# Another order for the half-size products of neighbouring units, and their follow-up work queued some products later

## The chip, the cores and the metric

The kernel is one program on one core of one Trainium2 chip. The metric is the device time of one execution in microseconds, from three runs; the profile is of one further execution. The engines are TensorE (PE in the profile, with its weight loads as PEld), VectorE (DVE), ScalarE (ACT), GpSimd (POOL) and SyncE (SP), which here issues all DMAs. Each engine takes its instructions in the order in which they stand.

## What is computed

One layer of an encoder block on 1024 tokens of width 2048, all in float32:

```python
h = rmsnorm(x, norm_w)
proj = einsum('bsd,de->bse', h, w_in)                # 2048 -> 5632
q_a, k_a, v_a, g_a, q_r, k_r, v_r, g_r = split(proj)
attn = windowed_attention(q_a, k_a, v_a, sink, rel_bias)   # 16 heads, +-128 tokens
attn = rmsnorm(attn, attn_out_norm_w) * silu(g_a)
ret = bidirectional_retention(rotary(q_r), rotary(k_r) * 64 ** -0.5, v_r, decays)  # 8 heads
ret = head_groupnorm(ret, ret_gn_w) * silu(g_r)
x = x + einsum('bse,ed->bsd', concat(attn, ret), w_out)    # 2048 -> 2048
out = rmsnorm(x, final_norm_w)
```

## The kernel before

**Two-part operands.** Every large matmul is done in three: each operand is split into a high part (`wh`, a cast by ACT) and the rest (`wl`, a subtraction, by POOL for the input weights and by DVE for the output weights), and high x high, high x low and low x high are added up in PSUM.

**Stages.** The work of PE stands in this order: six plain units (keys, values and queries of attention, list `STD`), 16 units with the half-size products (list `FAST`: per retention head pair `qk` and `vr`, four gates `ga` of attention, four gates `gr` of retention), done twice, and the output projection in eight column blocks. A unit is 256 output columns for all 1024 tokens. `q` counts the units of the second stage from 0 to 31: for `q` under `NF` = 16 the first half of the 2048 inputs, with the four results (tiles `e`, tags `e11` to `e22`) stored to `yd` in DRAM; from 16 on the second half, with the stored result loaded again as the start (`partial`).

**The half-size products.** A unit's 512 x 1024 half problem is done by seven products of half size (`p` = 0 to 6) instead of eight. Each is 12 matmuls (`multiply`): four rows of `hT`, which hold sums of the input made earlier (`combine`) and read back (`c_load`, `c_split`), times a weight block of 512 x 128. The blocks are the four raw ones (`raws`, loaded by `raw_load`) and their sums (`prep_sums`, on POOL in the first half and on DVE in the second); `prep` splits them. Products 0, 2, 4 and 5 accumulate in one PSUM bank (a, `psMa`), which is read after each; product 1 has bank b, and 3 and 6 have bank c (both `psMb`). `collect` reads a bank into a result tile `e`, by ACT or, in the second half, by an addition on DVE. `slots` lists the products of neighbouring units in turn:

```python
for qq, p in ((q, 0), (q - 1, 4), (q, 1), (q - 1, 6), (q, 2), (q - 1, 5), (q, 3)):
```

In the loop over `slots`, `prep` and `prep_sums` run two and three products ahead, then come `multiply`, `collect` and what is in the list `later`. A bank cannot take the next product before its reader is done.

**Follow-up work.** When a result is complete, `deliver` treats it by kind: a gate gets its SiLU on ACT, a `qk` block is rotated (a shuffle and two multiplications, on DVE and POOL, and an addition, functions `rope` and `add`), a `vr` block is transposed by PE (`to_tokens`). All are stored to DRAM (`gd`, `rqk`, `vrd`). The last two wait in `later` for one product.

**Other work in between.** Behind each three matmuls of the main work (and three of the plain and output units) `point()` counts on and takes steps of other work, at a pace in points: from `jobs` one step of attention or retention, from `aux` steps of smaller work, and it issues stores that are due. Attention (`attn_job`, four groups of four heads) starts in the last plain unit. Retention (`ret_job`, four head pairs) starts in unit `q` = 18; its steps contain the state scans (`kv`: many short DVE additions on `ST`) and the group norm (`o_mm`, `o_fin`). With it starts the premix (`premix`), which multiplies attention's rows by their norm and gate. In the last unit `mixed_load` and `mixed_row` begin to fill `hT` with the rows of the output projection.

Of the kernel before, what the change touches and what calls it, by code (L numbers as in the profile page):

```python
# [36 lines left out]
def hybrid_block(ctx: ExitStack, tc: tile.TileContext, a: dict, out: bass.AP):  # L37
# [93 lines left out]
    def w_low():  # L131
        return wp.tile([128, 512], F32R, tag="wl", name=nm("wl"), bufs=4)
# [66 lines left out]
    def w_load(i):  # L199
        if i < n_w[0] and i not in wraw and i not in wsp:  # L200
            r = et_(("e11", "e21")[i % 2] if i < W_STD else ("e11", "e22", "e21", "e12")[i % 4])
            SP.dma_start(r, w_src(i))
            wraw[i] = r
# [29 lines left out]
    pt, due, pace, adue, apace = [0], [0], [2.9], [0], [2.0]  # L233
# [260 lines left out]
    def attn_job(g):  # L494
# [47 lines left out]
        for t in range(32 + 8):  # L542
            if t < 32:
                b, c = divmod(t, 2)
                pr, n = divmod(b, 8)
                head = 4 * g + 2 * pr + c
                m0, m1 = max(n - 1, 0), min(n + 2, 8)
                W, k0 = 128 * (m1 - m0), 128 * (m0 - n + 1)
                q = qj[b // 2][:, c, 128 * (n % 2) : 128 * (n % 2) + 128]
                p = pS()  # L550
                T.matmul(p[:, :W], q, kh[:, 128 * m0 : 128 * m1], start=True, stop=False)
                T.matmul(p[:, :W], q, kl[:, 128 * m0 : 128 * m1], start=False, stop=True)  # L552
                if c == 0:
                    st[b] = tuple(small(2, w, 4) for w in ("nmx", "sums"))
                nmx, sums = st[b]

                x = att.tile([128, 388], F32, tag="P", name=nm("P"), bufs=5)
                V.tensor_copy(x[:, W : W + 1], nsink[:, head : head + 1])
                P[t] = x
                V.tensor_tensor_reduce(  # L560
                    x[:, :W], p[:, :W], bias[2 * pr + c][:, k0 : k0 + W], -1.0, nsink[:, head : head + 1],
                    ALU.add, ALU.min, nmx[:, c : c + 1],
                )
                A.activation(  # L564
                    x[:, : W + 1], x[:, : W + 1], AF.Exp, bias=nmx[:, c : c + 1], scale=-1.0, accum_out=sums[:, c : c + 1]
                )
                if c == 0 and b:
                    normalise(b - 1)
                if t in (4, 16):
                    load_bias(2 if t == 4 else 3)  # L570
                if t % 4 == 0 and t + 4 < 32:
                    q_load(t // 4 + 1)
            if t == 32:
                normalise(15)
            if t >= 6 and t % 2 == 0 and (t - 6) // 2 < 16:
# [9 lines left out]
                u = out_of(att, [128, 2, 128], F32, "u", 3)  # L585
# [3 lines left out]
            if t >= 4 and t - 4 < 32:  # L589
# [15 lines left out]
                tt(V, lo[:, :nk, c, :], p3, hi[:, :nk, c, :].bitcast(F32), ALU.subtract)  # L605
            yield

    def attn_sum(g):

        for kk in (2 * g, 2 * g + 1):  # L610
            for hf in range(2):
# [4 lines left out]
                yield  # L616
                yield
# [30 lines left out]
    def ret_job(p):  # L648
# [74 lines left out]
        def q_dec(ah):  # L723
            x = r4("qs")
            src = rq[64 * ah : 64 * ah + 64, :].rearrange("p (c i) -> p c i", c=8)
            for d in range(2):
                tt(G if d else V, x[64 * d : 64 * d + 64, :].rearrange("p (c i) -> p c i", c=8), src,
                   qd[64 * ah : 64 * ah + 64, d : d + 1, :].to_broadcast([64, 8, 128]), ALU.mult)
            QS[ah] = x

        def o_mm(ah, h, part):
# [3 lines left out]
            for c in (0, 1) if part == 0 else (2, 3):  # L735
                n = 4 * h + c
                T.matmul(o[:, 128 * c : 128 * c + 128], SD[ah, h][:, c, :], vsl(n, ah),
                         start=(c == 0), stop=False, skip_group_check=True)
                T.matmul(o[:, 128 * c : 128 * c + 128], QS[ah][:, 128 * n : 128 * n + 128],
                         ST[ah][:, 128 * n : 128 * n + 128], start=False, stop=True, skip_group_check=True)  # L740
# [15 lines left out]
        def o_fin(ah, h):  # L756
# [4 lines left out]
            stt(V, t, mv2[:, :, 0], -1.0, y, ALU.mult, ALU.mult)  # L761
            for c in range(4):
# [14 lines left out]
        for todo in (  # L777
            ((k_tr, 0), (q_dec, 0)),
# [9 lines left out]
            ((s_t, 1, 0),),  # L788
            ((o_fin, 0, 0), (o_mm, 0, 1, 0)),
            ((o_mm, 0, 1, 1),),  # L790
            ((o_tr, 0, 0), (kv, 1, 0), (q_dec, 1)),
            ((kv, 1, 1),),
            ((o_fin, 0, 1),),
            ((s_t, 1, 1),),
            ((o_tr, 0, 1),),
            ((o_mm, 1, 0, 0),),
            ((o_mm, 1, 0, 1),),
            ((o_mm, 1, 1, 0),),
            ((o_fin, 1, 0), (o_mm, 1, 1, 1)),
            (),  # L800
            ((o_tr, 1, 0), (o_fin, 1, 1)),
# [15 lines left out]
    def premix(kk):  # L817

        for hf in range(2):
# [4 lines left out]
            SP.dma_start(n, rbd[:, sl])  # L824
            yield
            yield
            tt(G, g, g, n, ALU.mult)
            yield
            yield
            stt(V, r, r, ew[:, kk : kk + 1], g, ALU.mult, ALU.mult)  # L830
            store(md[128 * kk : 128 * kk + 128, sl], r, r, (lambda: done.add(("pre", kk))) if hf else None)

    def mixed_load(kk, hf):
# [6 lines left out]
        mixing.append((kk, hf, r, g))  # L840

    def mixed_row():
        kk, hf, r, g = mixing.popleft()
        if g is not None:
            stt(V, r, r, ew[:, kk : kk + 1], g, ALU.mult, ALU.mult)
        row = 16 * hf + kk
        if row >= 28:
            omix[row] = (rt(F32R), rt(F32R))
        split(orow(row, 0), orow(row, 1), r)
# [32 lines left out]
    def c_split(r):  # L882
        split(hT[:, r, 0:512], hT[:, r, 512:1024], held(staged.pop(r), NT2))
# [37 lines left out]

    for u, (kind, i) in enumerate(STD):
        if u == 2:
            drain(aux, "rows")
        banks = [pS(), pS(), pT(), pO()] if u in (2, 4) else pM()
        st = []
        last_u = u == NS - 1
        for pos in range(NK):
# [21 lines left out]
            if last_u and pos >= 2:  # L950
                for r in range(2 * pos - 6, 2 * pos - 4):
                    if r >= 0:
                        c_split(r)
                for r in range(2 * pos - 4, 2 * pos - 2):
                    c_load(0, r)
            wh, wl = wsp[wi]
            first, last = pos == 0, pos == NK - 1
            for b in range(4):
                p = banks[b]
# [28 lines left out]

    raws, sums, ready_w, banks, outs = {}, {}, {}, {}, {}

    def raw_load(q, names):
        if q < 2 * NF:
            for x in names:
                raws[q, x] = rt(F32)
                SP.dma_start(raws[q, x], a["w_fast"][q, x])


    loads = {}
    for q in range(2 * NF):
        loads[q, 2], loads[q, 4] = [(q + 1, (0, 1))], [(q + 1, (2, 3))]  # L1000


    def prep_sums(q, p):
        eng = V if q >= NF else G
        if p == 2:
            s1, s2 = rt(F32), rt(F32)
            sums[q] = (s1, s2)
            tt(eng, s1, raws[q, 2], raws[q, 3], ALU.add)
            tt(eng, s2, s1, raws[q, 0], ALU.subtract)
        elif p == 4:  # L1010
            w2 = raws[q, 2]
            tt(eng, w2, raws[q, 0], w2, ALU.subtract)

    def prep(q, p):
        src = {0: raws[q, 0], 1: raws[q, 1], 4: raws.get((q, 2)), 5: raws.get((q, 3))}.get(p)
        if src is None:
            src = sums[q][0 if p == 3 else 1]
        hi, lo = wpair(q)
        split(hi, lo, src, G)
        ready_w[q, p] = (hi, lo)  # L1020
        if p == 2:

            tt(V if q >= NF else G, src, raws[q, 1], src, ALU.subtract)
        for at, names in loads.get((q, p), ()):
            raw_load(at, names)

    def multiply(q, p):
        if p in (0, 1, 3):
            banks[q, "abc"[(0, 1, 3).index(p)]] = psum("Ma" if p == 0 else "Mb", 2)
        bank = banks[q, {0: "a", 2: "a", 4: "a", 5: "a", 1: "b", 3: "c", 6: "c"}[p]]  # L1030
        wh, wl = ready_w.pop((q, p))
        for j in range(4):
            ws = slice(128 * j, 128 * j + 128)
            hh, hl = hT[:, 4 * p + j, 0:512], hT[:, 4 * p + j, 512:1024]
            T.matmul(bank, wh[:, ws], hh, start=(j == 0 and p in (0, 1, 3)), stop=False, skip_group_check=True)  # L1035
            T.matmul(bank, wh[:, ws], hl, start=False, stop=False, skip_group_check=True)  # L1036
            T.matmul(bank, wl[:, ws], hh, start=False, stop=(j == 3), skip_group_check=True)  # L1037
            point()

    later = deque()  # L1040

    def partial(q, b):

        if (q, b) not in outs:
            outs[q, b] = et_(("e11", "e12", "e21", "e22")[b])
            if q >= NF:
# [402 lines left out]
```

## Time and profile before

| | us |
|---|---|
| median of 3 runs | 1596.42 |
| lowest, highest | 1590.24, 1601.55 |
| the profiled execution | 1595.88 |
| its span in the profile | 1594.1 |
| mean granted PE clock | 0.975 |

The page of the profile gives the span, each engine's busy time and its share of it, the waits (who stood idle, and whose work ended the wait), and groups of instructions by line, engine, operation and tiles. The numbers behind names are left out there, so `psMb` is each tile of that tag. Most operations are recorded in small helpers (`tt` is L153, `stt` L156, the cast in `split` L159), so it is the tiles' names that tell them apart. L1035 to L1037 are the three matmuls of `multiply`, L1126 the transposes of `to_tokens`.

### The profile page before, as it was taken

The page shows a single profiled execution, that of the slowest core. Times are in us where ns is not written, and L with a number is a line of the kernel's source. Part 1 is how long each engine was busy: PE and PEld are TensorE (multiplying, and loading weights), DVE is VectorE, ACT ScalarE, POOL GpSimd, SP SyncE. Part 2 cuts the span into 40 slices and gives each one's busy share as a digit, 9 for nine tenths or more (in the row PEclk, how much of TensorE's full clock was granted, in tenths as well). Part 3 has the DMA queues.
Part 4 walks back from the last instruction along what each step waited for, and adds up shares of the span by engine and source line. Part 5 has one row for each costly group of instructions (what it writes and reads, how often), then busy time and mean ns, then how long its engine had stood idle before and what let it go on. Part 6 is the DMA issues. An engine that isn't in the chain of part 4 may idle for free. (4 is left out here: it accounts for less than half of the span.)

```text
span 1594.1 us, 21805 instructions
## 1 busy us (share of the span) xinstructions
PE 1484.5 (93%) x7250; PEld 1237.2 (78%) x7250; DVE 923.5 (58%) x1880; ACT 668.1 (42%) x1417; POOL 591.0 (37%) x457
## 2 busy tenths in 40 slices
PE   8999998999999999998888698879998999999997
PEld 6998877887888888887777577657777787887886
DVE  6655446854564664577747856867667444364323
ACT  5311136764675675774332232222353343333210
POOL 3232221446556556445645545554442000113000
PEclk9999999999999999999999899989999999999999
DMA  8888668775455556357774675675464565566413
GB/s 302 300 268 296 243 187 276 244 235 161 139 160 154 159 162 189 115 160 247 242 232 142 201 242 175 219 252 163 155 230 150 173 224 185 159 206 199 135 35 106
DMA packets 195405, 311.73 MB, mean 196 GB/s; under 512 B 29355, under 2 KB 67243, under 8 KB 194652
## 3 DMA queue, kind: packets, MB, share of 16 engines
q1 hardware_dynamic: 195292, 310.33, 60.0%
q8 instruction: 57, 0.93, 0.3%
q14 instruction: 56, 0.46, 0.1%
HBM read 216.38 MB, written 93.88 MB: 195 GB/s over the span
## 5 line engine op out<-in xcount | busy, mean ns | idle before, releaser
L153 POOL TENSOR_TENSOR wl<-r,wh 128x512 fp32r<-128x512 f32 x224 | 298.7, 1337 | 318.9 <-ACT wh L159 308.3
L159 ACT CAST wh<-r 128x512 fp32r<-128x512 f32 x224 | 138.3, 619 | 194.4 <-PE psMa L1036 82.7
L1035 PE MATMUL psMa<-hT,wh 128*128 128x512 f32 x512 | 213.1, 416 | 5.8 <-DVE e L153 4.0
L1037 PE MATMUL psMa<-hT,wl 128*128 128x512 f32 x512 | 201.7, 394 | 2.3 <-POOL wl L153 2.3
L1035 PE MATMUL psMb<-hT,wh 128*128 128x512 f32 x384 | 166.0, 432 | 38.8 <-DVE e L153 38.7
L1036 PE MATMUL psMa<-hT,wh 128*128 128x512 f32 x512 | 201.0, 393 | 0.0
L159 ACT CAST wh<-e 128x512 fp32r<-128x512 f32 x160 | 97.9, 618 | 216.7 <-PE psMb L1254 78.7
L153 DVE TENSOR_TENSOR wl<-e,wh 128x512 fp32r<-128x512 f32 x112 | 84.6, 761 | 132.4 <-ACT wh L159 127.9
L1036 PE MATMUL psMb<-hT,wh 128*128 128x512 f32 x384 | 157.6, 410 | 0.0
L1037 PE MATMUL psMb<-hT,wl 128*128 128x512 f32 x384 | 157.2, 409 | 0.0
L153 POOL TENSOR_TENSOR wl<-e,wh 128x512 fp32r<-128x512 f32 x48 | 71.9, 1501 | 203.8 <-ACT wh L159 203.8
L1035 PEld LDWEIGHTS psMb<-hT,wh 128*128 128x128 f32 x384 | 77.4, 202 | 56.0 <-issue 32.2
L1035 PEld LDWEIGHTS psMa<-hT,wh 128*128 128x128 f32 x512 | 96.9, 189 | 24.6 <-issue 3.4
L1037 PEld LDWEIGHTS psMa<-hT,wl 128*128 128x128 f32 x512 | 96.7, 189 | 24.4 <-POOL wl L153 2.7
L560 DVE CUSTOM_DVE_ANT_0 P<-psST,bias,nsink 128x384 f32<-128x384 f32 (+1 forms) x128 | 74.1, 580 | 62.7 <-PE psST L552 62.4
L1036 PEld LDWEIGHTS psMa<-hT,wh 128*128 128x128 f32 x512 | 97.3, 190 | 16.0
L153 DVE TENSOR_TENSOR PTl<-psST,PTh 128x384 fp32r<-128x384 f32 (+1 forms) x128 | 66.7, 521 | 45.5 <-ACT PTh L604 42.4
L153 POOL TENSOR_TENSOR r<-r,r 128x512 f32<-128x512 f32 x64 | 85.0, 1329 | 20.8 <-DMA yd<-e 6.7
L159 ACT CAST hT<-t 128x512 fp32r<-128x512 f32 x100 | 60.6, 620 | 72.0 <-DMA t<-in_w_out 25.5
L1037 PEld LDWEIGHTS psMb<-hT,wl 128*128 128x128 f32 x384 | 76.8, 200 | 17.7
L564 ACT ACTIVATE P<-P,nmx 128x385 f32<-128x385 f32 (+1 forms) x128 | 76.1, 594 | 30.5 <-DVE nmx L560 28.9
L153 DVE TENSOR_TENSOR e<-psMb,e 128x512 f32<-128x512 f32 x96 | 65.6, 686 | 38.9 <-PE psMb L1037 32.4
(335 smaller groups left out, 3530.3 us busy)
## 6 DMA issues: line engine op xcount, KB each, us to landing
r<-in_w_fast SPq DMA_DIRECT2D x128, 256.0 KB, 2.8
e<-in_w_out SPq DMA_DIRECT2D x112, 256.0 KB, 2.9
yd<-e SPq DMA_DIRECT2D x64, 256.0 KB, 2.9
e<-yd SPq DMA_DIRECT2D x64, 256.0 KB, 3.5
t<-in_xT SPq DMA_DIRECT2D x31, 512.0 KB, 6.1
t<-cd SPq DMA_DIRECT2D x56, 256.0 KB, 4.3
e<-in_w_in SPq DMA_DIRECT2D x48, 256.0 KB, 4.7
md<-t SPq DMA_DIRECT2D x48, 256.0 KB, 2.8
```

The source lines that it names most:

```text
L153: eng.tensor_tensor(o, x, y, op)
L159: A.copy(o_hi, x)
L560: V.tensor_tensor_reduce(x[:, :W], p[:, :W], bias[2 * pr + c][:, k0 : k0 + W], -1.0, nsink[:, head : head + 1], ALU.add, ALU.min, nmx[:, c ...
L564: A.activation(x[:, : W + 1], x[:, : W + 1], AF.Exp, bias=nmx[:, c : c + 1], scale=-1.0, accum_out=sums[:, c : c + 1])
L1035: T.matmul(bank, wh[:, ws], hh, start=(j == 0 and p in (0, 1, 3)), stop=False, skip_group_check=True)
L1036: T.matmul(bank, wh[:, ws], hl, start=False, stop=False, skip_group_check=True)
L1037: T.matmul(bank, wl[:, ws], hh, start=False, stop=(j == 3), skip_group_check=True)
```

## The change

The order of products within `slots` changes, with the order of `FAST`. Each bank is now read right behind its product (c after 3, where it had been read together with a after 4). `prep` and what is queued run in the middle of a product (`between`), and a queue with due slots (`lag`, `run_later`) replaces `later`. Weight sums are formed in place in three parts, at products 0, 6 and 4, with raw loads one by one. The premix moves to POOL; the rows of the output projection are gated by POOL and scaled by ACT's cast. An attention step begins with its last parts, a retention step is cut finer, and the paces become 2.7 (attention) and 2.75 with 2.3 for small work (retention). Some tiles have another number of buffers.

```diff
-FAST = []
-for _p in range(4):
-    FAST += [("qk", _p), ("vr", _p)]
-    FAST += [("ga", 2 * _p), ("ga", 2 * _p + 1)] if _p < 2 else []
-FAST += [("gr", _p) for _p in range(4)]
+FAST = [("ga", 0), ("qk", 0), ("vr", 0), ("qk", 1), ("vr", 1), ("ga", 1), ("qk", 2), ("vr", 2)]
+FAST += [("qk", 3), ("vr", 3), ("ga", 2), ("ga", 3)] + [("gr", _p) for _p in range(4)]
...
-        return out_of(com, [128, 512], F32, tag, 2 if tag == "e12" else 1)
+        return out_of(com, [128, 512], F32, tag, 2 if tag in ("e11", "e12") else 1)
...
-        return wp.tile([128, 512], dt, tag="r", name=nm("r"), bufs=8)
+        return wp.tile([128, 512], dt, tag="r", name=nm("r"), bufs=9)
...
-        return wp.tile([128, 512], F32R, tag="wl", name=nm("wl"), bufs=4)
+        return wp.tile([128, 512], F32R, tag="wl", name=nm("wl"), bufs=3)
...
-    pt, due, pace, adue, apace = [0], [0], [2.9], [0], [2.0]
+    pt, due, pace, adue, apace = [0], [0], [2.7], [0], [2.0]
...
             tt(G, g, g, n, ALU.mult)
-            yield
-            yield
-            stt(V, r, r, ew[:, kk : kk + 1], g, ALU.mult, ALU.mult)
+            tt(G, r, r, g, ALU.mult)
+            yield
...
+        if part == 0:
+            sums[q] = rt(F32)
+            tt(eng, raws[q, 0], raws[q, 0], raws[q, 2], ALU.subtract)
+            tt(eng, sums[q], raws[q, 3], raws[q, 0], ALU.subtract)
+        elif part == 1:
+            tt(eng, raws[q, 2], raws[q, 2], raws[q, 3], ALU.add)
+        else:
+            tt(eng, sums[q], raws[q, 1], sums[q], ALU.subtract)
...
+    def run_later(everything=False):
+        for _ in range(len(later)):
+            at, f = later.popleft()
+            if everything or at <= slot[0]:
+                f()
+            else:
+                later.append((at, f))
...
+        elif p == 3:
+            take(3, bc)
+        elif p == 4:
+            more(3, ba)
...
+            lag(1, gate)
...
+            lag(2, rope)
+            lag(3, add)
...
+            lag(2, to_tokens)
...
-        for qq, p in ((q, 0), (q - 1, 4), (q, 1), (q - 1, 6), (q, 2), (q - 1, 5), (q, 3)):
+        for qq, p in ((q, 0), (q, 1), (q - 1, 6), (q, 2), (q - 1, 5), (q, 3), (q, 4)):
...
+        def between():
+            if n + 2 < len(slots):
+                prep(*slots[n + 2])
+            run_later()
+
+        multiply(q, p, between)
+        collect(q, p)
...
-            pace[0], apace[0] = 3.5, 3.0
+            pace[0], apace[0] = 2.75, 2.3
```

Three places show what moves. The first is DVE's order in a `qk` unit of the second half, while retention runs; `e` are results, `psMa` and `psMb` banks, `r` weights and their sums. Before:

```order
L153 TENSOR_TENSOR e_1976_9231<-psMa_8939,e_1976_9231 128x512
L153 TENSOR_TENSOR r_9289<-r_9033,r_9289 128x512
L153 TENSOR_TENSOR e_1976_9231<-psMb_9202,e_1976_9231 128x512
L153 TENSOR_TENSOR e_1970_9200<-psMb_9316,e_1970_9200 128x512
L153 TENSOR_TENSOR e_1940_9068<-psMb_9202,e_1940_9068 128x512
```

DVE, the same place of a unit in the changed kernel (the shuffle and the two `t` rows are a rotation, `bny` and `bnt` the group norm):

```order
L150 TENSOR_TENSOR e_1980_9318<-psMb_9401,e_1980_9318 128x512
L150 TENSOR_TENSOR bny_9389<-bny_9389,bnt_9440 128x4
L153 SCALAR_TENSOR_TENSOR bnt_9440<-bmv_9376,bny_9389 128x4
L150 TENSOR_TENSOR e_1980_9318<-psMa_9201,e_1980_9318 128x512
L1070 STREAM_SHUFFLE t_2006_9464<-e_1980_9318 128x512
L150 TENSOR_TENSOR e_1992_9399<-psMa_9468,e_1992_9399 128x512
L150 TENSOR_TENSOR t_2006_9464<-t_2006_9464,t_2005_9460 128x512
L150 TENSOR_TENSOR r_9465<-r_9314,r_9465 128x512
L150 TENSOR_TENSOR e_1980_9318<-e_1980_9318,t_2006_9464 128x512
L150 TENSOR_TENSOR e_1992_9399<-psMb_9492,e_1992_9399 128x512
L150 TENSOR_TENSOR e_1958_9237<-psMb_9401,e_1958_9237 128x512
```

Before, bank c (`psMb_9202`) is read together with product 4's bank a and again, with product 6 in it, after one other product's read (`psMb_9316`). Now the two reads of `psMb_9401` have those of three products between them.

The second place is PE around the transposes of a value result. Before, where `e_1976` is complete when bank `psMa_8939` has been read (the rows left out are the rest of one product's 12):

```order
L1037 MATMUL psMa_8939<-hT,wl_9193 128x512
L1035 MATMUL psMb_9316<-hT,wh_9227 128x512
...
L1037 MATMUL psMb_9316<-hT,wl_9228 128x512
L1035 MATMUL psMa_9233<-hT,wh_9307 128x512
L1126 MATMUL psST_9349<-ident,e_1976_9231 128x128 x4
L1035 MATMUL psMb_9202<-hT,wh_9284 128x512
```

PE in the changed kernel, where `e_1915` is complete when bank `psMa_8658` has been read (L697 is a retention step; left out are the rest of a product and most of half a product):

```order
L983 MATMUL psMa_8658<-hT,wl_9008 128x512
L981 MATMUL psMb_9109<-hT,wh_9040 128x512
...
L697 MATMUL psST_9147<-vt_8671,kT_8779 128x128 x4
L981 MATMUL psMa_8916<-hT,wh_9068 128x512
...
L983 MATMUL psMa_8916<-hT,wl_9069 128x512
L1086 MATMUL psST_9177<-ident,e_1915_8999 128x128 x4
```

The transposes stood one product behind their result and ahead of the next use of a bank; they now stand one and a half products behind it, in the middle of a product.

The third place is the premix. Before, its second multiplication (by `ew`) stands in DVE's order between weight sums and a bank's read; the two sums overwrite weights which POOL's split has just read:

```order
L153 TENSOR_TENSOR r_9288<-r_9196,r_9198 128x512
L153 TENSOR_TENSOR r_9196<-r_9031,r_9196 128x512
L156 SCALAR_TENSOR_TENSOR t_1943_9085<-t_1943_9085,ew,t_1944_9086 128x512
L153 TENSOR_TENSOR e_1940_9068<-psMa_8939,e_1940_9068 128x512
L1107 STREAM_SHUFFLE t_1955_9137<-e_1881_8771 128x512
```

POOL in the changed kernel, at the start of retention (`wl` are low parts of the weights):

```order
L150 TENSOR_TENSOR t_1792_8408<-t_1792_8408,t_1793_8409 128x512
L150 TENSOR_TENSOR wl_8437<-r_8337,wh_8436 128x512
L150 TENSOR_TENSOR t_1791_8407<-t_1791_8407,t_1792_8408 128x512
L150 TENSOR_TENSOR wl_8463<-r_8252,wh_8462 128x512
L150 TENSOR_TENSOR t_1803_8474<-t_1803_8474,t_1804_8475 128x512
L150 TENSOR_TENSOR t_1802_8473<-t_1802_8473,t_1803_8474 128x512
L150 TENSOR_TENSOR wl_8491<-r_8452,wh_8490 128x512
```

Both multiplications now stand between the low parts on POOL, and none on DVE.

More of the change, by code (lines that the diff above doesn't have):

```diff
@@ L839, in mixed_load, with mixed_rows @@
             SP.dma_start(g, gd[128 * kk : 128 * kk + 128, sl])
[L840 to L849, printed above, removed]
+        mixing.append([kk, hf, r, g])
+    def mixed_rows(keep):
+        for m in list(mixing)[: max(len(mixing) - 1, 0) if keep else None]:
+            if m[3] is not None:
+                tt(G, m[2], m[2], m[3], ALU.mult)
+                m[3] = None
+        while len(mixing) > keep:
+            kk, hf, r, _ = mixing.popleft()
+            row = 16 * hf + kk
+            if row >= 28:
+                omix[row] = (rt(F32R), rt(F32R))
+            c = ew[:, kk : kk + 1]
+            A.activation(orow(row, 0), r, AF.Copy, scale=c)
+            stt(V, orow(row, 1), r, c, orow(row, 0).bitcast(F32), ALU.mult, ALU.subtract)
     def evac(u, b, p, st):
@@ new lines, in prep, with multiply @@
+    def prep(q, p):
+        src = {0: 0, 1: 1, 3: 2, 4: 0, 5: 3}.get(p)
+        src = sums[q] if src is None else raws[q, src]
+        hi, lo = wpair(q)
+        split(hi, lo, src, G)
+        ready_w[q, p] = (hi, lo)
+    def multiply(q, p, between):
+        if p in (0, 1, 3):
+            banks[q, "abc"[(0, 1, 3).index(p)]] = psum("Ma" if p == 0 else "Mb", 2)
+        bank = banks[q, {0: "a", 2: "a", 4: "a", 5: "a", 1: "b", 3: "c", 6: "c"}[p]]
+        wh, wl = ready_w.pop((q, p))
+        for j in range(4):
+            ws = slice(128 * j, 128 * j + 128)
+            hh, hl = hT[:, 4 * p + j, 0:512], hT[:, 4 * p + j, 512:1024]
+            T.matmul(bank, wh[:, ws], hh, start=(j == 0 and p in (0, 1, 3)), stop=False, skip_group_check=True)
+            T.matmul(bank, wh[:, ws], hl, start=False, stop=False, skip_group_check=True)
+            T.matmul(bank, wl[:, ws], hh, start=False, stop=(j == 3), skip_group_check=True)
+            if j == 1:
+                between()
+            point()
@@ new lines, in collect, with take, more @@
+    def collect(q, p):
+        ba, bb, bc = (banks.get((q, c)) for c in "abc")
+        def take(b, bank):
+            o = partial(q, b)
+            if q >= NF:
+                tt(V, o, bank, o, ALU.add)
+            else:
+                A.copy(o, bank)
+        def more(b, bank):
+            tt(V, outs[q, b], bank, outs[q, b], ALU.add)
+            deliver(q, b)
+        if p == 0:
+            take(0, ba)
+        elif p == 1:
+            more(0, bb)
+        elif p == 2:
+            take(1, ba)
+        elif p == 3:
+            take(3, bc)
+        elif p == 4:
+            more(3, ba)
+        elif p == 5:
+            take(2, ba)
+            deliver(q, 2)
+        elif p == 6:
+            more(1, bc)
@@ L922, in hybrid_block @@
+    slots = []
+    for q in range(2 * NF + 1):
+        for qq, p in ((q, 0), (q, 1), (q - 1, 6), (q, 2), (q - 1, 5), (q, 3), (q, 4)):
+            if 0 <= qq < 2 * NF:
+                slots.append((qq, p))
+    LAST = 2 * NF - 1
     for u, (kind, i) in enumerate(STD):
@@ L1014, in prep @@
[L1014 to L1038, printed above, removed]
```

359 lines of the change are left out of this document (170 added, 189 removed).

## The prediction

> **What bounds the kernel now.** I read the page first, then the busy time by stage, then what TensorE waited for, then two of those waits row by row. The page gives the span and the shares:
>
> ```profile
> span 1594.1 us, 21805 instructions
> PE 1484.5 (93%) x7250; PEld 1237.2 (78%) x7250; DVE 923.5 (58%) x1880; ACT 668.1 (42%) x1417; POOL 591.0 (37%) x457
> ```
>
> TensorE (PE) is busy 1484.5 of 1594.1 us, and the change adds no matmul. So the kernel can only win what PE loses: 109.6 us of idle time, and the time in which it ran at a lower clock. The view by stage says where (after each stretch its length, then the busy time of PE, weight loads, VectorE (DVE), ScalarE (ACT) and GpSimd (POOL), then PE's granted clock, the DMA share and GB/s):
>
> ```profile
> 301.50:712.50 411.00, 401.19 (x2080) 342.55 (x2079) 233.89 (x625) 265.71 (x636) 233.56 (x180) 0.99 0.52 164
> 712.50:837.50 125.00, 110.09 (x514) 88.92 (x513) 83.57 (x111) 49.47 (x92) 63.71 (x47) 0.97 0.75 242
> 837.50:1213.40 375.90, 320.80 (x1555) 263.22 (x1554) 268.07 (x519) 121.64 (x234) 182.24 (x142) 0.93 0.60 197
> 1262.50:1540.90 278.40, 275.03 (x1205) 225.18 (x1204) 125.06 (x195) 94.64 (x183) 24.12 (x20) 1.00 0.54 173
> ```
>
> The half-size products run from 301.5 to 1213.4. While attention runs among them (first row) PE lacks 9.8 us. Behind it PE lacks 14.9 and then, with the retention steps, 55.1 us, and there the clock falls to 0.93. The output projection (last row) is full. DVE is busy 268 of 376 us in the poor stage, so the trouble is lateness in bursts and not a full engine. Who is late is in the view of PE's waits (us in total, times, longest):
>
> ```profile
> PE psMb L1035 <- DVE e L153: 38.7, 10, 5.7
> PE psST L1126 <- DVE e L153: 22.5, 7, 7.7
> PE psMa L1035 <- DVE e L153: 4.0, 3, 2.8
> PE psMa L1037 <- POOL wl L153: 2.3, 1, 2.3
> ```
>
> The first and third are a product that waits until DVE has read its PSUM bank: 42.7 us in 13 waits. The second is a transpose that waits for a finished result. Together 65.2 us. One wait in order of time, PE above and DVE below:
>
> ```profile
> 836.80 0.39 PE L1035 MATMUL psMa<-hT,wh 128*128 128x512 f32 x1
> 837.03 0.39 PE L1036 MATMUL psMa<-hT,wh 128*128 128x512 f32 x1
> ...
> 841.34 0.39 PE L1037 MATMUL psMb<-hT,wl 128*128 128x512 f32 x1
> 846.11 0.77 PE L1035 MATMUL psMb<-hT,wh 128*128 128x512 f32 x1 [4.39 <-DVE e L153]
> 846.67 0.63 PE L1036 MATMUL psMb<-hT,wh 128*128 128x512 f32 x1
> 847.10 0.63 PE L1037 MATMUL psMb<-hT,wl 128*128 128x512 f32 x1
> ```
>
> ```profile
> 837.21 1.76 DVE L156 SCALAR_TENSOR_TENSOR t<-t,ew,t 128x512 f32<-128x512 f32 x1 [3.72 <-POOL t L153]
> ...
> 845.27 0.69 DVE L153 TENSOR_TENSOR e<-psMb,e 128x512 f32<-128x512 f32 x1
> ```
>
> DVE first stood 3.72 us in front of a premix multiplication whose input POOL had not finished. It then worked without a pause through that, the state scan and two other result additions, and read the bank only at 845.27; PE, which had only one product of cover, stood from 841.7 to 846.1. It came back at half speed: a matmul each 0.43 us (846.67 to 847.10) where it had been 0.23 (836.80 to 837.03). How DVE falls behind is in its own waits from 712 to 1213 us:
>
> ```profile
> DVE r L153 <- POOL wl L153: 27.9, 13, 7.2
> DVE t L156 <- POOL t L153: 23.2, 8, 5.8
> DVE bnt L153 <- POOL bny L153: 17.5, 13, 3.5
> DVE e L153 <- POOL e L153: 8.8, 8, 1.2
> DVE hT L153 <- ACT hT L159: 7.5, 6, 3.2
> ```
>
> These five are 84.9 us in which DVE, which takes its rows in order, held back every bank read queued behind.
>
> **The change part by part.** The page's run took 1595.88 us, 1.8 above its span; the median of the three runs is 1596.42. I sum against 1595.9.
>
> *The order of products.* A product is 12 matmuls, 12 x 0.227 = 2.7 us. Before, the third bank (c) was read after product 4 and used again with one product between; now it is read after product 3, and no bank has fewer than two between. Bank a keeps fewer than it had (two for three), so the gain is one product on the shortest cover, not on each. If DVE stays as late as it is, each of the ten long waits (mean 3.9 us) keeps 3.9 - 2.7 = 1.2 us, so 12 us remain of 42.7. If the 84.9 us go, next to nothing remains. I take the middle: 6 remain, **36.7 us** go.
>
> *Follow-up queued later.* The transposes of a value result came one product after the result; now one and a half. If lateness stays, the mean wait of 22.5 / 7 = 3.2 us loses 1.36 and 13 us remain; if it goes, nothing. I take 7, so **15.5 us** go. The same queue puts the rope's last addition a product behind POOL's multiplication, the low half of a copied row a product behind ACT's cast, and the norm's Newton steps one step later; the third weight sum now comes well after the split that reads its old value; the premix goes to POOL altogether. That covers each of the five rows above.
>
> *The clock.* In the stage at 0.93, half-speed time is 2 x 0.07 x 375.9 = 53 us. If the stage's 55 us of idle all lay inside this time, nothing was lost to it; if none did, 0.07 x 320.8 = 22. The rows at 846 us show that PE works at half speed after the wait, not during it, so I take 20. The 13 us of waits that remain of 65.2 keep a fifth of it: **16 us** go.
>
> [...]
>
> *Preparing the weights.* The split of the weights two products on (ACT's cast, POOL's subtraction) is now issued in the middle of a product instead of ahead of it. Its rows, and those of the operations that change engine (busy, mean ns, then the idle time before them), from 712 to 1213 us:
>
> ```profile
> L159 ACT CAST wh<-r 128x512 fp32r<-128x512 f32 x116 | 71.3, 619 | 148.7 <-PE psMa L1036 65.2 <-PE psMb L1036 63.4 <-issue 8.5
> L153 POOL TENSOR_TENSOR wl<-r,wh 128x512 fp32r<-128x512 f32 x117 | 158.6, 1362 | 158.4 <-ACT wh L159 155.4 <-DMA gd<-e 1.5 <-issue 1.2
> L153 POOL TENSOR_TENSOR t<-t,t 128x512 f32<-128x512 f32 x16 | 21.2, 1327 | 30.8 <-DMA t<-rbd 16.4 <-DMA t<-gd 6.4 <-DMA r<-in_w_fast 6.3
> L156 DVE SCALAR_TENSOR_TENSOR t<-t,ew,t 128x512 f32<-128x512 f32 x22 | 25.1, 1143 | 23.5 <-POOL t L153 23.2 <-DMA t<-gd 0.2
> L153 DVE TENSOR_TENSOR r<-r,r 128x512 f32<-128x512 f32 x64 | 57.3, 900 | 36.2 <-POOL wl L153 27.9 <-DMA r<-in_w_fast 7.6
> L153 DVE TENSOR_TENSOR e<-psMb,e 128x512 f32<-128x512 f32 x52 | 35.4, 685 | 22.6 <-PE psMb L1037 21.9
> ```
>
> The split takes 0.62 + 1.36 = 2.0 us and now has 1.5 x 2.7 = 4.1 us until its product starts, a margin of 2.1 (3.4 before). The cast's old wait for PE to free the buffer (128.6 us of ACT) goes with it; it cost PE nothing, since PE released it. A premix half now puts two POOL multiplications, 2.66 us, in the queue, 0.6 over the margin: sixteen halves give at most 9 us if none waits for its load, and 16 x (0.6 + 2.3) = 46 if each still waits the 16.4 / 7 = 2.3 us of the row; the lower end is 0. The loads now get three steps of the queue instead of two, and a low part often stands between the two multiplications, so I stay near the 9 and take **+6 us**.
>
> *The loads.* Raw weights are now loaded one at a time, at three places of a unit:
>
> ```profile
> SPq L995 <- POOL r L153: 62.4, 28, 4.2
> r<-in_w_fast SPq DMA_DIRECT2D x128, 256.0 KB, 2.8
> ```
>
> SP issues in order, so a load that waits for its buffer holds back the stores and loads behind it, 62.4 us in this row alone. Each load now comes two products or more after the last reader of its buffer was issued, and its first use two products or more later: 5.4 us against 2.8 to land. I count 0; if SP were over 2.6 us late, DVE's sums would be late by the rest, which is part of the first rival.
>
> *At nothing.* The order of units, the earlier start of the first weight loads, one more buffer for weights and for one partial result, the split of the query decay into halves, and the output's six weight tiles move no PE work, and PE's own products cover them (401 of 411 and 275 of 278 us busy). One buffer less for the low weight half makes three, as many as the high half has. Attention's tighter pace (2.7 points, where a point is three matmuls of the main work) falls in a stage where PE lacks 9.8 us in all: 0, bounds 10 us both ways, and the buffer fewer of its two tile kinds is within them. Retention's pace goes from 3.5 to 2.75: the same PE work earlier, its DVE rows denser; that is a rival below. Its last steps leave the stretch from 1213 us, which gains or loses 3 us at most.
>
> The sum: 36.7 + 15.5 + 16 - 6 = 62, so 1595.9 - 62 = **1534 us**.
>
> **The rivals.** *DVE still late in bursts* (18%). Retention has eight state scans, and they come 3.5 / 2.75 = 1.27 times as dense. If each still stops PE for 4.5 us (the wait above was 4.39) and costs 2.3 of clock, 8 x 6.8 = 54 us remain of 65.2 + 20; with 6 for POOL the gain is 25, **1571 us**. For it: the run of DVE rows behind 837.21 has no gap. Against: it began with the 3.72 us that go.
>
> *POOL slows DVE* (8%). DVE's additions with both inputs in SBUF take 900 ns where those from PSUM take 685, so something holds them. POOL gets 16 more premix products and 8 of the gate; if each holds a DVE row for half its 1.33 us, that is 16 us, with the clock loss 21: **1555 us**. [...]
>
> *The weights come late* (6%, slower). With less room, the low half misses its product each time. If the queue ahead of each split is over 2.1 us on average, the half product taken away, 1.36 us, is paid by the 112 products of the second half: 152 us against the 85 saved, **1663 us**. For it: POOL would be busy (182 + 24 x 1.33) of 314 us there, 68% where it was 48%. Against: before, PE waited for a low half once, 2.3 us.
>
> *Nothing changes* (6%): the time lost moves to the next late reader, **1596 us**.
>
> **How the numbers follow.** My forecast has 62%, with a range of its own from 1500 (all of 65.2 + 22 and 9 of attention's idle gone) to 1560 (12 and 13 remain, clock 12, POOL 15). The range 1500 to 1580 takes in the first two rivals and leaves out the last two and the upper end of POOL's 46 us. The three runs lie within 0.4% of their median, so about 1% can be told from no change. Below 1580 lie the forecast, the first two rivals less a little: faster 0.86, same 0.07, slower 0.07.
>
> **What would show it.** Right: PE's waits for DVE's bank reads fall from 42.7 to under 15 us and the transposes' from 22.5 to under 10; DVE's five waits fall below 20 us; the clock from the end of attention to the end of the products is 0.97 or more; the products end near 1150 us. Wrong: a row PE <- POOL wl of over 20 us (the third rival), waits for DVE of over 4 us beside state scans (the first), or DVE's two-input additions well above 900 ns (the second).

## The result and the profile after

| | before | changed |
|---|---|---|
| median, us | 1594.03 (4 runs, 1590.24 to 1601.55) | 1575.64 (4 runs, 1573.45 to 1579.63) |
| changed / before | | 0.988, interval 0.984 to 0.993 |
| profiled execution, us | 1595.88 | 1579.63 |
| its span, mean granted PE clock | 1594.1, 0.975 | 1577.9, 0.978 |

The changed kernel is 18 us faster, where 62 were forecast: less than a third. The direction is the forecast one, and the time is inside the range, near its upper end. The page of the changed kernel gives the shares:

```profile
span 1577.9 us, 22010 instructions
PE 1485.4 (94%) x7250; PEld 1233.9 (78%) x7250; DVE 896.2 (57%) x1856; ACT 675.1 (43%) x1417; POOL 639.3 (41%) x497
```

PE's idle time went from 109.6 to 1577.9 - 1485.4 = 92.5 us. PE's busy time is the same, and DVE has 27 us less work. So the result lies in how long PE stood idle. The view by stage, with the columns of before, says where they went:

```profile
303.80:718.00 414.20, 406.91 (x2126) 345.94 (x2125) 239.78 (x640) 276.29 (x653) 233.36 (x179) 1.00 0.54 169
718.00:840.00 122.00, 115.12 (x537) 93.60 (x536) 87.35 (x113) 46.11 (x82) 83.77 (x59) 0.99 0.81 265
840.00:1196.70 356.70, 313.22 (x1549) 255.85 (x1548) 246.42 (x520) 125.24 (x241) 196.22 (x160) 0.94 0.62 196
1248.00:1524.00 276.00, 264.93 (x1132) 214.00 (x1131) 109.41 (x170) 87.60 (x169) 34.83 (x28) 0.98 0.50 157
```

The half-size products now end at 1196.7 instead of 1213.4, where 1150 was expected. PE lacks 6.9 us in the second row, after 14.9. The stage with the retention steps (third row) still lacks 43.5 us, after 55.1, and its clock is 0.94, after 0.93. The output projection (last row) was full. It now lacks 11.1 us, and its clock is 0.98 where it was 1.00. From the end of the products to the end of the span it is 381.2 us, as before (380.7), though the first three rows hold 63 matmuls more than before (4212 after 4149), which this stretch no longer has to do. PE's waits (total, times, longest):

```profile
PE psO L738 <- DVE ST L153: 26.2, 7, 7.1
PE psST L1086 <- DVE e L150: 6.3, 3, 2.9
PE psMb L983 <- POOL wl L150: 6.0, 5, 2.1
PE psST L1295 <- ACT wh L156: 4.9, 3, 2.6
PE psMb L981 <- DVE bnt L153: 4.3, 1, 4.3
PE psMa L981 <- DVE e L150: 3.9, 2, 2.6
PE psMa L1295 <- ACT wh L156: 3.9, 2, 3.6
PE psMa L983 <- POOL wl L150: 2.0, 3, 0.9
```

The waits that the change is about went: the banks (L981) from 42.7 to 4.3 + 3.9 = 8.2 us, and the transposes (L1086) from 22.5 to 6.3. The row that names `bnt` is a bank wait: a second profiled execution of the same kernel puts that single wait, 4.5 us there, down to the bank's reader `e`. In their place stands the top row. L738 is `o_mm`, the matmul of retention that reads the state `ST`, and the state scan on DVE is late for it: 26.2 us where it had been 2.1, in this row of the kernel before:

```profile
PE psO L739 <- DVE ST L156: 2.1, 1, 2.1
```

The two rows at L1295 are the output projection, which waits for the high parts of its weights: 8.8 us where it had been 0.2.

One of the seven waits for the scan, in order of time, PE above and DVE below:

```profile
844.18 0.38 PE L736 MATMUL psO<-vt,sd 128*128 128x128 f32 x2
850.54 0.80 PE L738 MATMUL psO<-ST,qs 128*128 128x128 f32 x2 [5.98 <-DVE ST L153]
851.13 0.64 PE L736 MATMUL psO<-vt,sd 128*128 128x128 f32 x2
...
852.41 0.63 PE L982 MATMUL psMa<-hT,wh 128*128 128x512 f32 x1
852.84 0.63 PE L983 MATMUL psMa<-hT,wl 128*128 128x512 f32 x1
```

```profile
836.77 1.75 DVE L150 TENSOR_TENSOR e<-e,t 128x512 f32<-128x512 f32 x1 [0.58 <-POOL e L150]
838.55 0.56 DVE L707 COPY ST<-psST 64x384 f32<-64x384 f32 x1
...
843.17 0.69 DVE L709 COPY ST<-psST 64x512 f32<-64x512 f32 x1
...
850.13 0.35 DVE L153 SCALAR_TENSOR_TENSOR ST<-ST,cdec 64x128 f32<-64x128 f32 x1
```

From 836.77 on DVE works without a pause through two scans, and bank reads, a rotation and weight sums stand between the scan's rows. The last row of the scan ends at 850.5, and only then `o_mm` starts. Here DVE is late by its own work. Another wait, 300 us further on, has a longer chain, on POOL, DVE and PE:

```profile
1126.04 2.66 POOL L150 TENSOR_TENSOR t<-t,t 128x512 f32<-128x512 f32 x2 [5.20 <-DMA t<-rbd]
1132.53 2.64 POOL L150 TENSOR_TENSOR t<-t,t 128x512 f32<-128x512 f32 x2 [2.59 <-DMA t<-rbd]
```

```profile
1141.52 4.09 DVE L150 TENSOR_TENSOR r<-r,r 128x512 f32<-128x512 f32 x3 [6.95 <-POOL wl L150]
```

```profile
1151.26 0.80 PE L738 MATMUL psO<-ST,qs 128*128 128x128 f32 x2 [7.06 <-DVE ST L153]
```

POOL stands in front of two premix products whose load has not come, 5.20 and 2.59 us. The low parts `wl` queued behind them come late. DVE may not overwrite the weights in place until POOL has read them, and stands 6.95 us. The scan queued behind it is late, and PE stands 7.06 us. DVE's waits from 712 to 1213 us show how much of this there is:

```profile
DVE r L150 <- POOL wl L150: 50.8, 18, 7.0
DVE bnt L150 <- POOL bny L150: 15.2, 15, 2.3
DVE e L150 <- POOL e L150: 6.4, 6, 2.4
```

The wait for the premix is gone from DVE (23.2 to 0), but the wait of the weight sums has grown from 27.9 to 50.8. With 2.1 us for ScalarE's high part of a copied row, the five rows are 74.5 us, after 84.9.

### The profile page after: what moved, and what is told of

Same layout as the page of the kernel before. It is cut to its first block, busy times and chain, and to the rows that moved or that the text cites. A ratio compares the mean times of both kernels' runs of the same rounds, so it can differ in the third digit from the quotient of the medians.

```text
span 1577.9 us, 22010 instructions
## 1 busy us (share of the span) xinstructions
PE 1485.4 (94%) x7250; PEld 1233.9 (78%) x7250; DVE 896.2 (57%) x1856; ACT 675.1 (43%) x1417; POOL 639.3 (41%) x497
## 5 line engine op out<-in xcount | busy, mean ns | idle before, releaser
L150 POOL TENSOR_TENSOR wl<-r,wh 128x512 fp32r<-128x512 f32 x224 | 302.4, 1356 | 287.9 <-ACT wh L156 278.3
L981 PE MATMUL psMa<-hT,wh 128*128 128x512 f32 x512 | 209.9, 410 | 4.4 <-DVE e L150 3.9
L981 PE MATMUL psMb<-hT,wh 128*128 128x512 f32 x384 | 156.5, 408 | 4.3 <-DVE bnt L153 4.3
L983 PE MATMUL psMb<-hT,wl 128*128 128x512 f32 x384 | 152.9, 398 | 6.1 <-POOL wl L150 6.0
L982 PE MATMUL psMb<-hT,wh 128*128 128x512 f32 x384 | 151.9, 396 | 0.0
L150 POOL TENSOR_TENSOR t<-t,t 128x512 f32<-128x512 f32 x48 | 64.5, 1345 | 134.1 <-DMA t<-gd 102.3
L981 PEld LDWEIGHTS psMa<-hT,wh 128*128 128x128 f32 x512 | 98.4, 192 | 22.4 <-issue 4.7
L983 PEld LDWEIGHTS psMb<-hT,wl 128*128 128x128 f32 x384 | 73.2, 191 | 24.9 <-POOL wl L150 8.7
L150 DVE TENSOR_TENSOR r<-r,r 128x512 f32<-128x512 f32 x64 | 61.8, 977 | 51.2 <-POOL wl L150 50.8
L981 PEld LDWEIGHTS psMb<-hT,wh 128*128 128x128 f32 x384 | 73.5, 191 | 17.7 <-issue 4.9
L982 PEld LDWEIGHTS psMb<-hT,wh 128*128 128x128 f32 x384 | 73.3, 191 | 12.4
```

The lines of the kernel that those rows point to most:

```text
L150: eng.tensor_tensor(o, x, y, op)
```

## The experiments

The theory was: (A) the scan is given fewer points before `o_mm` reads it, and DVE is as late as before, so `o_mm` now waits where a bank did; (B) the gate product on POOL blocks ScalarE's scaled cast and with it the output weights' high parts; (C) the premix pair on POOL delays the low parts and through them DVE. The main rival to each was that DVE is late by a fixed amount, so that what is taken from one reader goes to the next and the time stays.

The distance in (A) shrank in two ways. A retention job treats two heads one after the other. From the last scan step of the first head to its `o_mm` there are three steps in both kernels: 3 x 3.5 = 10.5 points before, 3 x 2.75 = 8.25 now. For the second head there were four steps, 14 points. In the finer list of steps there are three, 8.25 points.

All ratios are against the kernel before, run on the same chip. The changed kernel was run again beside the first three experiments, as their yardstick.

> The changed kernel once more, as the mark for the others on the same chip. Every theory: 0.988 of the kernel before, within 0.4%.

Measured: 1578.5 us, 0.988 (0.986 to 0.990), with the same waits (scan 28.0 us, transposes 6.9, banks 4.5 and 4.3).

**Room for the scan (A).** Two empty steps ahead of each head's first `o_mm`, and the pace tightened so that retention ends at the same place as in the changed kernel (5 x 2.46 = 12.3 points for each head):

```diff
             (),
             (),
+            (),
+            (),
             ((o_mm, 0, 0, 0),),
...
+            (),
+            (),
             ((o_mm, 1, 0, 0),),
...
-            pace[0], apace[0] = 2.75, 2.3
+            pace[0], apace[0] = 2.46, 2.3
```

> The changed kernel with two empty retention steps more between the second state scan and the first product that reads it, for both heads, and the pace 2.46 instead of 2.75 points so that retention ends at the same place. Theory (the wait of 26.2 us of TensorE for the state scan took the place of the bank waits): that wait falls under 8 us and the kernel is 15 to 25 us faster than the changed one. Rival (VectorE is late anyway, because its weight sums wait for GpSimd's low parts): the wait moves to bank reads or transposes and the kernel stays within 6 us of the changed one.

Measured: 1563.24 us, 0.979 (0.977 to 0.981), 15.3 us under the yardstick. Four of PE's waits and the stage in this kernel:

```profile
PE psST L1090 <- DVE e L150: 12.6, 5, 5.3
PE psMa L985 <- DVE e L150: 6.4, 3, 2.9
PE psO L738 <- DVE ST L153: 5.9, 4, 1.8
PE psMb L985 <- DVE e L150: 2.7, 1, 2.7
```

```profile
840.00:1196.70 356.70, 320.49 (x1610) 260.45 (x1609) 253.21 (x538) 129.34 (x251) 198.65 (x162) 0.97 0.62 198
```

The wait for the scan fell from 28.0 to 5.9 us, and the clock in the stage rose from 0.94 to 0.97. The theory is borne out. The rival is right in part: the transposes took back 5.7 of the 22 us. Transposes and banks together wait 12.6 + 9.1 = 21.7 us here, where they waited 15.7 in the yardstick.

**The gate product on VectorE (B).** The row of the output projection is gated and scaled by one DVE operation, as before the change. One loaded row is kept waiting instead of two, also as before:

```diff
-                tt(G, m[2], m[2], m[3], ALU.mult)
...
-        while len(mixing) > keep:
...
+        while len(mixing) > min(keep, 1):
...
+            if g is not None:
+                stt(V, r, r, c, g, ALU.mult, ALU.mult)
+                split(orow(row, 0), orow(row, 1), r)
+                continue
```

Why ScalarE is held shows in the changed kernel's waits from 1197 to 1330 us, ScalarE's two rows above POOL's:

```profile
ACT r L862 <- POOL t L150: 21.7, 4, 6.6
ACT hT L862 <- POOL t L150: 21.2, 5, 5.6
```

```profile
POOL t L150 <- DMA t<-gd: 93.7, 9, 35.6
```

ScalarE's cast waits for POOL's product, POOL's product for a load, and the weights' casts stand behind on ScalarE.

> The changed kernel with the gate of the projection's rows multiplied by VectorE right before the split, as before the change, instead of by GpSimd ahead of ScalarE's scaled cast. Theory (ScalarE stands in front of its scaled casts until GpSimd has the product, and the output weights behind it are late): ScalarE's waits of 43 us for GpSimd there go, TensorE's 8.8 us of waits for the cast of output weights fall under 2, and the kernel is 8 to 13 us faster than the changed one. Rival (those loads are late whoever multiplies): within 4 us of the changed kernel.

Measured: 1566.74 us, 0.980 (0.977 to 0.982), 11.8 us under the yardstick. The output stage, and what ScalarE waits for there (1180 to 1340 us):

```profile
1248.00:1524.00 276.00, 270.13 (x1176) 219.44 (x1176) 114.51 (x180) 84.72 (x166) 24.38 (x20) 1.00 0.50 156
```

```profile
ACT hT L156 <- DVE t L153: 23.8, 8, 4.8
ACT r L156 <- DVE t L153: 13.3, 3, 5.8
```

The clock there is 1.00 again and PE waits 0.9 us for `wh`, after 8.8, while the wait for the scan is as it was (26.2 us). So this is a loss of its own. ScalarE's waits were expected to go and did not: 37.1 us on DVE stand in place of 42.9 on POOL. Why they no longer reach PE is not shown, and with two changes in the edit neither is shown alone.

**The second premix product on VectorE (C).** As before the change, the last of the two multiplications is DVE's, two steps behind POOL's:

```diff
-            for _ in range(3):
+            for _ in range(2):
                 yield
             tt(G, g, g, n, ALU.mult)
-            tt(G, r, r, g, ALU.mult)
-            yield
+            for _ in range(2):
+                yield
+            tt(V, r, r, g, ALU.mult)
```

> The changed kernel with the second premix product on VectorE again, two steps behind GpSimd's first. Theory (the premix on GpSimd makes the low parts late, and VectorE's weight sums wait for them): VectorE's wait for low parts falls from 50.8 to about 30 us, TensorE's from 8.0 to about 4, and the wait for the premix product comes back with some 15 us; the time stays within 6 us of the changed kernel. Rival (moving the premix was the gain): 15 us or more slower than the changed kernel.

Measured: 1572.54 us, 0.985 (0.982 to 0.988), 6.0 us under the yardstick. The intervals overlap (0.9855 to 0.9879), so this one alone is not beyond doubt. DVE's waits from 712 to 1213 us:

```profile
DVE r L150 <- POOL wl L150: 26.6, 15, 3.0
DVE t L150 <- POOL t L150: 19.7, 10, 3.5
```

The wait of the weight sums halves (50.8 to 26.6), and the premix is waited for again, 19.7 us. PE waits 2.7 + 2.6 us for low parts, after 6.0 + 2.0. The move to POOL is no source of the gain.

**All three together.** This is the changed kernel with the three edits above.

> The changed kernel with the three edits together: room behind the state scans, the row gate on VectorE, the second premix product on VectorE. If the three losses are apart from each other, the gains add up: 15 + 12 + 5 us, about 0.967 of the kernel before. Rival (each edit takes the same lateness of VectorE away): no better than 0.975.

Measured: 1545.88 us, 0.968 (0.964 to 0.972): the best version, 51.7 us under the kernel before (1597.56 on this chip), and faster than the changed kernel too. The three gains were 15.3 + 11.8 + 6.0 = 33.1 us alone. Together they are 32.6 against the yardstick, or 32 by the ratios (0.9878 - 0.9679), since this run was on another chip. The interval of this run is some 6 us either way, so the losses are separate as far as can be told, and the rival's 0.975 is out. The retention stage and the first waits:

```profile
840.00:1174.50 334.50, 304.60 (x1533) 247.61 (x1532) 247.78 (x523) 120.23 (x236) 177.46 (x141) 0.97 0.62 201
```

```profile
PE psST L1091 <- DVE e L150: 12.5, 6, 3.6
PE psO L738 <- DVE ST L153: 5.7, 4, 3.4
```

The products end at 1174.5 us, and none of these waits is over 4 us.

**One product between uses of bank a.** Products 4 and 3 are exchanged in the changed kernel, so that the bank of product 2 is used again by 4 with one product between, where the changed kernel has two, and bank c has two instead of three. The additions, sums and loads tied to the two products move with them:

```diff
-        for qq, p in ((q, 0), (q, 1), (q - 1, 6), (q, 2), (q - 1, 5), (q, 3), (q, 4)):
+        for qq, p in ((q, 0), (q, 1), (q - 1, 6), (q, 2), (q - 1, 5), (q, 4), (q, 3)):
...
```

> The changed kernel with products 4 and 3 of each unit exchanged, so that bank a has one other product between products 2 and 4 instead of two, and bank c two instead of three. Theory (the spacing of bank uses took the bank waits away): TensorE's waits for VectorE's bank reads rise from 8 us (bank a and b together) to 25 to 40, and the kernel is 15 to 30 us slower than the changed one. Rival (VectorE is less late now, the spacing does not matter): they stay under 12 us, and the kernel within 6 us of the changed one.

Measured: 1576.87 us, 0.988 (0.984 to 0.992), no different from the changed kernel.

```profile
PE psO L738 <- DVE ST L153: 19.8, 5, 7.1
PE psMa L981 <- DVE e L150: 10.1, 4, 3.7
PE psMb L981 <- DVE e L150: 5.3, 1, 5.3
```

The banks cost 15.4 us, 7 more than in the changed kernel, which lies between the two forecasts, and the scan 6.4 less. The rival is right on the time: the wait at the banks rose by about what the wait for the scan fell.

**Transposes one product sooner.** `to_tokens` is queued one place instead of two, so half a product behind the result. This is closer than in the kernel before, where it was one product:

```diff
-            lag(2, to_tokens)
+            lag(1, to_tokens)
```

> The changed kernel with the transposes of value results half a product behind the result instead of one and a half. Theory (the queue of follow-up work took their wait away): TensorE's wait for results at the transposes rises from 6.3 us to 30 or more, 16 results by 2 us or more, and the kernel is 20 to 30 us slower than the changed one. Rival: it stays under 15 us.

Measured: 1597.84 us, 1.000 (0.997 to 1.002): the whole gain is gone. (The profiled execution, 1588.7 us, is the fastest of its ten.)

```profile
PE psST L1086 <- DVE e L150: 32.2, 9, 5.7
PE psO L738 <- DVE ST L153: 13.4, 4, 5.1
```

The transposes wait 26 us more and the scan 13 less. So this place of the transposes costs about 19 us, just under the 20 to 30 expected. What the step from one product to one and a half was worth was not run alone.

**Bank c read late.** The changed kernel, but product 3's bank is read with a after product 4 again and used again with one product between:

```diff
-        for qq, p in ((q, 0), (q, 1), (q - 1, 6), (q, 2), (q - 1, 5), (q, 3), (q, 4)):
+        for qq, p in ((q, 0), (q - 1, 6), (q, 1), (q, 2), (q - 1, 5), (q, 3), (q, 4)):
...
-        elif p == 3:
-            take(3, bc)
         elif p == 4:
-            more(3, ba)
+            take(3, ba)
+            more(3, bc)
...
```

The third weight sum and one load of a partial result move by a product with it.

> The changed kernel with bank c read as before the change: together with bank a after product 4, and used again by product 6 with one other product between (products 1 and 6 of neighbouring units exchanged). Theory (reading c right behind product 3, three products ahead of its next use, took the bank waits away): TensorE's waits for VectorE's bank reads rise from 8 us to 25 to 40, and the kernel is 15 to 30 us slower than the changed one. Rival (VectorE is less late, and the new wait for the state scan would have come in any order): they stay under 15 us, and the time within 6 us.

Measured: 1591.27 us, 0.997 (0.995 to 0.999), about 14 us over the changed kernel (0.009 x 1596).

```profile
PE psMb L981 <- DVE e L150: 32.0, 10, 6.3
PE psO L738 <- DVE ST L153: 17.3, 5, 5.7
```

The bank's ten waits are back, 32.0 us after 38.7 before the change, while the scan waits 9 us less than in the changed kernel and the transposes 6 less. The time is just under the 15 to 30 us of the theory and outside the rival's 6. So bank c, read early and used again late, carries the reorder, with the reservation that the sum and the load moved too.

**The kernel before with the new pace.** Nothing but the paces of retention:

```diff
-            pace[0], apace[0] = 3.5, 3.0
+            pace[0], apace[0] = 2.75, 2.3
```

> The kernel before with the new pace of retention and small work alone (2.75 and 2.3 points). Theory (the pace is what makes TensorE wait for the state scan): TensorE's wait for the scan rises from 2.1 us to 8 or more beside the old bank waits of 40 us, which stay or grow, and the kernel is no faster than before, 0 to 15 us slower. Rival (the pace is harmless, the steps' new order is the cause): the wait stays under 4 us and the time within 5 us.

Measured: 1605.32 us, 1.005 (1.003 to 1.008), 8 us slower.

```profile
PE psST L1126 <- DVE e L153: 16.9, 6, 5.4
PE psMa L1035 <- DVE e L153: 13.0, 5, 7.6
PE psO L739 <- DVE ST L156: 11.8, 5, 3.8
PE psMb L1035 <- DVE e L153: 11.4, 4, 3.3
```

The wait for the scan rose from 2.1 to 11.8 us by the pace alone. In order of time, 10.3 us of it fall on the first heads (8.25 points) and 1.5 on the second heads, which still have four steps (11 points). In the changed kernel 16.3 of the 26.2 us fall on the first heads and 9.9 on the second, which have three steps there. So the pace explains part of the wait, and the step that the second heads lost most likely another part; no run gave that step back alone. That the banks' waits fell to 24.4 (from 42.7) was not expected. On the whole the waits only changed places: PE's idle time is 109.0 us, after 109.6, and its busy time rose from 1484.5 to 1495.8 us at a mean clock of 0.972. The tighter pace alone gains nothing, and the loss is in slower matmuls; why they are slower with as much idle time stays open.

**Transposes one product later still.** The best version with `lag(3, to_tokens)`, after its largest remaining row:

```diff
-            lag(2, to_tokens)
+            lag(3, to_tokens)
```

> The three mended edits with the transposes another product later (three instead of two). Theory (TensorE's 12.5 us at the transposes are VectorE's bursts, and more distance covers them): that wait falls under 4 us, the kernel is 6 to 12 us faster than with the three edits, about 0.962 of the kernel before. Rival (the lateness moves to the next reader): within 3 us of the three edits, with bank waits of over 15 us.

Measured: 1554.4 us, 0.973 (0.971 to 0.975), 8 us slower than the best version (the intervals touch, 0.9707 to 0.9716).

```profile
PE psO L738 <- DVE ST L153: 19.4, 5, 7.3
```

The transposes' 12.5 us go to nothing, and the scan's wait comes back with 19.4 us. The rival is right that the next reader pays, but the reader is the scan and not the banks (7.2 us), and it pays more than was saved.

## Why the prediction was right and wrong

Of the five signs of being right two came: the waits for bank reads (8.2 us) and at the transposes (6.3). DVE's five waits (74.5 us), the clock behind attention (0.99 and then 0.94 beside retention) and the end of the products (1196.7 us) missed.

**Right in number: the order of products.** 34.5 us of bank waits went, 36.7 were forecast. That bank c is the part that counts is borne out by reading it late (32.0 us of waits, some 14 us of time), while one product less between the uses of bank a changed no time.

**Right in number: the transposes.** 16.2 us went, 15.5 were forecast, and queuing them a product sooner costs some 19 us.

Both numbers were hit in part by luck. They are middles between a case in which DVE stays late (12 + 13 = 25 us remain) and one in which it does not. DVE stayed late: 74.5 of 84.9 us. With the wait for the scan mostly gone (A), banks and transposes wait 21.7 us, near the first case; in the changed kernel PE stood at the scan instead, and they wait 14.5.

**Right in number: the low parts on POOL.** PE's wait for them went from 2.3 to 8.0 us, +5.7 where +6 was forecast; in a second execution of the same kernel it was 6.1 us. With the second premix product off POOL it was 5.3.

**Wrong: the retention pace "at nothing".** It was counted as the same PE work earlier, with the denser DVE rows left to the first rival. That rival described this mechanism (waits of over 4 us beside state scans, clock still low; 1571 us), and its time is the nearest to the result. But it took its price from a bank wait and did not ask who reads the scan: the wait came at `o_mm`. Its distance had shrunk from 10.5 points to 8.25 for the first heads, by the pace, and from 14 to 8.25 for the second, by the pace and a step fewer, which the prediction does not mention. The cost was 26.2 - 2.1 = 24.1 us of waiting; giving room back brought 15.3 us of time.

**Wrong: the output stage "at nothing".** "275 of 278 us busy" was taken as cover. It showed that nothing was late there, not how much room there was: the row's gate went from DVE to POOL, where it stands behind loads, and ScalarE's cast, behind which the weights' casts are queued, stood for it. PE waited 8.8 us there and the clock fell to 0.98; undone, 11.8 us of time.

**Wrong: "the third weight sum now comes well after the split".** It does in the order of work, but POOL, with the premix on it, reads the weights late, and the wait grew from 27.9 to 50.8 us. So DVE's five rows did not fall below 20 us but to 74.5, and the source of the lateness stayed. With the second premix product back on DVE the wait is 26.6 us, so it is that move that raised it; the time gained is about 6 us, at the edge of the noise.

**Wrong by size: the clock.** 16 us were forecast. By the mean clock, the loss over the whole span went from 0.025 x 1594.1 = 39.9 to 0.022 x 1577.9 = 34.7, some 5 us as an estimate. PE's busy time for the same 7250 matmuls shows none of it: 1484.5 and 1485.4 us. The clock rose by 0.01 beside retention and fell by 0.02 in the output stage. In these traces the drop goes with long waits. From 700 to 1310 us PE had nine of 3.6 to 7.7 us before the change and has six of 3.6 to 7.1 us after it. Behind each of them the matmuls start some 0.43 us apart (852.41 to 852.84 above), where 0.23 is usual. With room for the scan one is left (5.3 us) and the clock beside retention rises to 0.97, the kernel's to 0.986. With all three edits none is left, and the kernel's is 0.988.

The length of a wait alone does not decide it. Waits of 2.56, 2.87 and 2.63 us (at 745, 924 and 1280 us of the changed kernel) are also followed by matmuls 0.43 us apart, one of 3.23 us (at 740 us before the change) is followed by the usual 0.23, and one of 3.57 us in the version with all three edits (at 1000 us) is not followed by slower matmuls either. What else decides it is not shown.

The profiles add up as follows. The waits named here sum to -34.5 - 16.2 + 5.7 + 24.1 + 8.6 = -12.3 us. PE's idle time fell by 17.1 us, so some 5 us went in smaller waits that were not followed. The busy time rose by 0.9, and the spans differ by 16.2.

**Rivals not met.** The weights did not come late as a rule (8.0 us in all). The additions of the weights on DVE take 977 ns after 900 (the mean in the row below), worth 64 x 0.077 = 5 us of DVE where the second rival had 16. That POOL is the cause is not shown: with the second premix product off POOL the mean is 869 ns, but with all three edits, which take more off POOL, it is 958.

```profile
L150 DVE TENSOR_TENSOR r<-r,r 128x512 f32<-128x512 f32 x64 | 61.8, 977 | 51.2 <-POOL wl L150 50.8
```

**Open.** The best version still stands 12 us above the forecast of 1534. Its 12.5 us of transposes, 24.5 us of weight sums waiting for POOL and a clock of 0.97 beside retention were not taken apart further. Of the terms put at nothing, the order of units, attention's pace, the loads one by one and the numbers of buffers were not run alone; the stage with attention lacks 7.3 us where it lacked 9.8.

## What to carry to other kernels

VectorE took its work in order here and was late in bursts, and whoever came next waited: 42.7 us at the banks before the change, 26.2 us at the scan after it, 32.2 us at the transposes when they were queued sooner. Moving one reader back without removing the lateness can hand the wait to another (bank, transposes and scan traded it in five runs here). So list every consumer of an engine that is late in this way, and its distance in steps and in points, before a pace is tightened or a list of steps is cut anew. And before an operation moves to another engine, look at what stands ahead of it there (a load) and at what stands behind its consumer: a stage that is fully busy shows that nothing is late, not that there is room (275 of 278 us busy before the change, 8.8 us of waits for the weights' casts after it).

## What was not expected of the hardware

Nearly half of what room for the scan won came after the waits. Behind the 5.98 us wait the same pair of matmuls (L736) took 0.64 us where it had taken 0.38. When room for the scan took 22 us of such waits away, PE's idle time fell only from 91.9 to 83.3 us (others grew), but its busy time fell too, from 1485.6 to 1478.2 us for the same 7250 matmuls: 7.4 of the span's 16.0 us were matmuls that ran faster.

A GpSimd product that waited for its load held what stood behind it on that engine: at 1126 and 1132 us the premix stood 5.20 and 2.59 us, the low parts behind it came late, and VectorE stood 6.95 us. On one of the premix's loads GpSimd stood 28.7 us in all in the profiled execution, 18.0 in a second one of the same kernel (16.4 before the change), and on the gates' loads of the output projection 93.7 us.
